# Attention weights turned by VectorE in blocks of 32 and placed by DMA over memory instead of by TensorE, key copies made by DMA, and eight weight sums moved to later units

## The chip, the cores and the metric

The kernel runs on one core of one Trainium2 chip. The metric is the device time of one execution in microseconds (us). A core has a matrix engine (TensorE, PE in the profile, with its weight loads shown apart as PEld), a vector engine (VectorE, DVE), a scalar engine (ScalarE, ACT), GpSimd (POOL), and SyncE (SP), which issues nearly all DMAs here. Each engine works through its own list of instructions strictly in order; an instruction that waits holds up all those behind it on that engine.

## What is computed

One encoder block on 512 positions of width 2048, in float32. The normalised input is projected once; half of the columns feed an attention of 16 heads of 64, the other half a gated linear attention of 4 heads. Both are gated, put together, projected again, added to the input and normalised. What matters here is the attention part, cut to its core:

```python
for window, dilation in DILATED_PATTERNS:      # (128,1), (512,4), (2048,16)
    o_p, lse_p = dilated_window_attention(aq, ak, av, rel_bias, window, dilation)
...
mix_w = jax.nn.softmax(jnp.stack(lses, axis=0), axis=0)
att = jnp.einsum('pbsh,pbshe->bshe', mix_w.astype(av.dtype), jnp.stack(outs, axis=0))
a_out = att.reshape(B, S, ATT_WIDTH) * jax.nn.silu(ag)
```

The three patterns merged by their denominators are one softmax over all 512 keys with a bias that depends on the distance alone, so for each head P = softmax(QK' + bias), a 512 x 512 matrix, and the output is P V.

## The kernel before

**Products.** A float32 product is made of three passes with rounded operands: each operand is split into a high part (ScalarE rounds it) and a low part (VectorE subtracts), and `three` (lines 169 to 171) does high x high, high x low and low x high. One call of `three`, three matmuls of 512 columns, is called a *tick* below.

**Units.** After a start stage the projection runs in *units* (`unit`): `qk2`, `qk4`, `qk6`, `gk`, `gv0`, `gv1`, `ag0`, `ag1`, `gg0`, `gg1`, then the output projection `o0` to `o3`. A unit has 64 ticks into four PSUM banks, in eight groups of eight, a group for each 512 KB of weights. A group's weights come by DMA into one of four `raw` buffers (line 286), ScalarE makes the high part (line 313) and VectorE the low part (line 297). `unit` takes a list of side work with places between 0 and 1; a piece is issued after the tick that its place names, and pieces with a place of 1 or more go to the next unit. TensorE's order is exactly the order of the code (`manual_schedule(engines={E.PE})`). The other engines' orders are chosen by the framework's scheduler when the program is built, piece by piece, among what it holds to be ready; side work is raised in priority (`urgent`).

**Attention as side work.** Four units (`qk2`, `qk4`, `qk6`, `gk`) carry four heads each, 16 tiles of 128 queries. Names in the orders below: `s13` are the scores of head 1, tile 3; `p13` its P; `pt01` the turned P of head 0, half 1 (tiles 2 and 3); `o01` the product of that half with V. For each tile:

- `score` (lines 567 to 587): two matmuls (576, 577), then VectorE adds the bias and takes the extreme (580), ScalarE the exponential with its sum (583), VectorE the reciprocal (584), GpSimd the scaling of P (585).
- `turn` (589 to 603): TensorE turns P against the identity in four 128 x 128 pieces (597) into a PSUM bank, ScalarE takes the high part (601), VectorE the low part (602), 512 columns each.
- `values` (605 to 619), once for two tiles: eight matmuls of 256 columns (611) with high and low part, a ScalarE copy (614), a VectorE addition into `cat` (618).

The side list is score x, turn x-1, values of the pair that ended with x-2, evenly spaced by `ATT_AT`. Scores, turned P and products share three PSUM banks.

**Keys.** At a unit's end `qk_evict` (line 531 on) takes queries and keys out of PSUM for the next unit's heads. A head's keys are wanted in both halves of the 128 partitions, so ScalarE copies the high part twice (548, 549) and VectorE makes the low part twice (550, 551), 64 x 512 each.

**Sums.** 48 pieces of weights (512 KB each, also through the `raw` buffers) are multiplied by a row and summed on VectorE (lines 244 and 680, about 1.3 us a piece). `SUMS_IN` says how many go into which unit; the rest fall into `gg1`.

## Time and profile before

| | |
|---|---|
| median of 3 runs | 975.26 us (973.75 to 977.06) |
| profiled execution, its own time | 973.38 us |
| span of its trace | 971.6 us |
| TensorE busy over the span | 943.0 us, 97% |
| VectorE, ScalarE, GpSimd busy | 616.6, 441.0, 81.6 us |
| first tick of `qk2` to first tick of `gv0` (four attention units) | 192.2 to 473.5 us |
| `gv0` and `gv1` | 473.5 to 580.6 us |

Times in the profile are from the span's start. A row of the timeline has start, duration, engine, line, operation, output and inputs; in brackets the idle time before it and what ended that. A matmul's duration is longer than its distance to the next one, since matmuls overlap: the distance of two starts is what one costs. The chain of waits counts that distance.

### The profile page before, as it was taken

The page shows a single profiled execution, that of the slowest core. Times are in us where ns is not written, and L with a number is a line of the kernel's source. Part 1 is how long each engine was busy: PE and PEld are TensorE (multiplying, and loading weights), DVE is VectorE, ACT ScalarE, POOL GpSimd, SP SyncE. Part 2 cuts the span into 40 slices and gives each one's busy share as a digit, 9 for nine tenths or more (in the row PEclk, how much of TensorE's full clock was granted, in tenths as well). Part 3 has the DMA queues.
Part 4 walks back from the last instruction along what each step waited for, and adds up shares of the span by engine and source line. Part 5 has one row for each costly group of instructions (what it writes and reads, how often), then busy time and mean ns, then how long its engine had stood idle before and what let it go on. Part 6 is the DMA issues. An engine that isn't in the chain of part 4 may idle for free.

```text
span 971.6 us, 11885 instructions
## 1 busy us (share of the span) xinstructions
PE 943.0 (97%) x4464; PEld 775.7 (80%) x4464; DVE 616.6 (63%) x916; ACT 441.0 (45%) x735; POOL 81.6 (8%) x100
## 2 busy tenths in 40 slices
PE   8999999989999999999999999999999999999996
PEld 4888788878778777778777888888888888888884
DVE  7988999566665676775534647585885352546431
ACT  5443533655655645655413544363744151333222
POOL 0000000011111122012000000000010000202120
PEclk9999999999999999999999999999999999999998
DMA  9998687422222253332444334355465455244013
GB/s 333 414 411 347 238 302 258 133 85 96 92 84 82 85 193 105 126 128 84 146 152 166 121 109 152 130 176 171 139 228 176 152 175 193 87 148 156 22 50 124
DMA packets 42619, 159.56 MB, mean 164 GB/s; under 512 B 5217, under 2 KB 5505, under 8 KB 37825
## 3 DMA queue, kind: packets, MB, share of 16 engines
q1 hardware_dynamic: 42386, 158.48, 47.2%
q8 instruction: 35, 0.57, 0.2%
q10 hardware_dynamic: 176, 0.33, 0.1%
q14 instruction: 22, 0.18, 0.1%
HBM read 154.51 MB, written 4.28 MB: 163 GB/s over the span
## 4 chain that ended last, share of the span: by engine, by line
PE 81%; DVE 8%; DMA 3%; ACT 3%; issue 3%; POOL 1%; SPq 0%; ACTq 0%; DVEq 0%; POOLq 0%
PE ps_o L170 6%; PE ps_o L171 6%; PE ps_o L169 6%; PE sta L169 3%; PE sta L170 3%; PE sta L171 3%; PE stb L171 3%; PE stb L169 3%; PE stb L170 3%; PE ps_qk L169 3%; PE ps_gv L170 3%; PE ps_gv L171 3%; PE ps_gv L169 3%; PE ps_qk L171 3%; PE ps_qk L170 3%
## 5 line engine op out<-in xcount | busy, mean ns | idle before, releaser
L585 POOL TENSOR_SCALAR p<-p,st 128x512 f32<-128x512 f32 x64 | 46.1, 721 | 424.3 <-DVE st L584 407.8
L583 ACT ACTIVATE p<-p,st 128x512 f32<-128x512 f32 x64 | 46.2, 722 | 63.4 <-DVE st L580 63.4
L244 DVE CUSTOM_DVE_ANT_0 cb<-cb,sb,c_bcond 128x2048 f32<-128x2048 f32 (+1 forms) x32 | 73.4, 2294 | 0.0
L602 DVE TENSOR_TENSOR pt<-t,pt 128x512 fp32r<-128x512 f32 x64 | 44.1, 689 | 17.8 <-ACT pt L601 17.8
L597 PE MATMUL t<-c_ident,p 128*128 128x128 f32 x256 | 38.9, 275 | 10.6 <-POOL p L585 10.6
L597 PEld LDWEIGHTS t<-c_ident,p 128*128 128x128 f32 x256 | 30.9, 140 | 22.3 <-POOL p L585 15.4
L580 DVE CUSTOM_DVE_ANT_0 p<-s,g 128x512 f32<-128x512 f32 x64 | 43.6, 686 | 7.0 <-PE s L577 6.1
L601 ACT ACTIVATE pt<-t 128x512 fp32r<-128x512 f32 x64 | 37.8, 591 | 21.1 <-PE t L597 20.5
L244 DVE CUSTOM_DVE_ANT_0 rawg<-rawg,sb,gate 128x1024 f32<-128x1024 f32 x16 | 20.7, 1294 | 27.8 <-DMA rawg<-in_wg 27.8
L611 PEld LDWEIGHTS o<-pt,vv 128*128 128x128 f32 x256 | 34.2, 189 | 3.8 <-DVE pt L602 1.7
L244 DVE CUSTOM_DVE_ANT_0 rawg<-rawg,sb,c_bcond 128x1024 f32<-128x1024 f32 x16 | 20.5, 1283 | 25.2 <-DMA rawg<-in_wg 25.2
L611 PE MATMUL o<-pt,vv 128*128 128x256 f32 x256 | 35.9, 283 | 0.0
L1014 POOL TENSOR_TENSOR x<-x,fgain 128x512 f32<-128x512 f32 x12 | 20.0, 1675 | 183.8 <-ACT ysq L1012 183.8
L1012 ACT ACTIVATE ysq<-x 128x512 f32<-128x512 f32 x16 | 10.1, 632 | 47.1 <-DVE x L1010 44.8
L767 POOL TENSOR_SCALAR dc<-st,sc 128x256 f32<-128x256 f32 x16 | 10.5, 656 | 242.5 <-DVE st L764 237.6
L584 DVE RECIPROCAL st<-st 128x1 f32<-128x1 f32 x64 | 10.4, 162 | 31.3 <-ACT p L583 31.2
L1009 DVE TENSOR_TENSOR y<-ps_o,sb 128x512 f32<-128x512 f32 x16 | 10.9, 684 | 25.9 <-PE ps_o L171 25.9
L576 PE MATMUL s<-ks,qs 128*128 128x512 f32 x64 | 25.3, 395 | 0.2 <-DVE qs L540 0.2
L577 PE MATMUL s<-kl,qs 128*128 128x512 f32 x64 | 25.0, 391 | 0.0
L774 ACT ACTIVATE sq<-st,sc 128x256 f32<-128x256 f32 x24 | 12.2, 509 | 26.2 <-DVE st L769 13.8
L618 DVE TENSOR_TENSOR cat<-o,oh 64x256 f32<-64x256 f32 x32 | 13.3, 415 | 11.9 <-ACT oh L614 11.7
L614 ACT ACTIVATE oh<-o 64x256 f32<-64x256 f32 x32 | 12.2, 380 | 17.3 <-PE o L611 16.5
(1279 smaller groups left out, 2944.6 us busy)
## 6 DMA issues: line engine op xcount, KB each, us to landing
cb<-in_wm SPq DMA_DIRECT2D x31, 1024.0 KB, 7.5
rawg<-in_wg SPq DMA_DIRECT2D x32, 512.0 KB, 3.4
raw_o<-in_w_o SPq DMA_DIRECT2D x32, 512.0 KB, 3.4
raw_qk<-in_w_qk SPq DMA_DIRECT2D x24, 512.0 KB, 3.3
rawb<-in_w_sb SPq DMA_DIRECT2D x16, 512.0 KB, 4.3
rawv<-in_wv SPq DMA_DIRECT2D x16, 512.0 KB, 3.4
raw_gv<-in_w_gv SPq DMA_DIRECT2D x16, 512.0 KB, 3.4
raw_ag<-in_w_ag SPq DMA_DIRECT2D x16, 512.0 KB, 3.4
```

What stands on the lines that cost most here:

```text
L169: mm(ps, lh, rh, start=first, stop=False)
L170: mm(ps, ll, rh, start=False, stop=False)
L171: mm(ps, lh, rl, start=False, stop=last)
L244: nc.vector.tensor_tensor_reduce(out=w, in0=w, in1=with_, op0=ALU.mult, op1=ALU.add, scale=1.0, scalar=init, accum_out=dst)
L576: mm(ps, qs[:, q], ks, start=True, stop=False)
L580: nc.vector.tensor_tensor_reduce(out=t, in0=ps, in1=gt[h][:, P * i:P * i + 512], op0=ALU.add, op1=ALU.min, scale=1.0, scalar=3e38, accum_o ...
L583: act(t, t, AF.Exp, bias=st[:, 0:1], scale=-1.0, accum_out=st[:, 1:2])
L585: nc.gpsimd.tensor_scalar(t, t, st[:, 2:3], 1.0, op0=ALU.mult, op1=ALU.mult)
L597: nc.tensor.transpose(pk[:, kt * P:kt * P + P], t[:, kt * P:kt * P + P], ident)
L601: act(hi, src, AF.Copy)
L602: tt(lo, src, hi.bitcast(F32), op=ALU.subtract)
L611: mm(po[:, :256], vv[h // 4][:, kt, h % 4, :], t[:, w, kt, :], start=kt == 0 and w == 0, stop=kt == 3 and w == 1)
```

## The change

1. `score` ends after the exponential. Reciprocal and scaling become a piece of their own, `scale`.
2. `turn` no longer uses TensorE. VectorE turns P in blocks of 32 x 32 within SBUF (STREAM_TRANSPOSE, 128 x 512), and SP writes the result to a buffer in memory (`away`, 256 KB a tile).
3. A new piece `back`, once for two tiles: four DMAs on SP read the buffer in such an order that the blocks land on the right partitions (`pf`, in a `raw` buffer; 128 KB each, in runs of 512 bytes). It waits for the two writes.
4. A new piece `parts`, once for two tiles: high part on ScalarE and low part on VectorE, 1024 columns each, out of SBUF.
5. The side list has places of its own for each piece of tile x, in steps of 0.0525 of a unit from 0.14 on: score at x, scale at x + 0.45, turn at x + 1.05; for a pair that ends with x: back at x + 1.9, parts at x + 3.1, values at x + 4.2. The values of a unit's last two pairs fall into the next unit.
6. The second copies of the keys (549, 551) become DMAs within SBUF on SP.
7. `SUMS_IN`: no sums in `qk6` and `gk` (4 each before); `gv0` 12 (9), `gv1` 5 (2), `ag0` 8 (7), `gg1` 5 (4). One more buffer of the `t2` pool, less scratch for DMAs.

```diff
-ATT_AT = (0.17, 0.8, 0.04, 0.05, 0.05)
+ATT_AT = (0.14, 0.0525)
-SUMS_IN = {"qk6": 4, "gk": 4, "gv0": 9, "gv1": 2, "ag0": 7, "ag1": 9, "gg0": 9}
+SUMS_IN = {"gv0": 12, "gv1": 5, "ag0": 8, "ag1": 9, "gg0": 9}
...
-            act(ks[oth], psk[own], AF.Copy)
+            nc.sync.dma_start(ks[oth].bitcast(F32), ks[own].bitcast(F32))
             tt(kl[own], psk[own], ks[own].bitcast(F32), op=ALU.subtract)
-            tt(kl[oth], psk[own], ks[own].bitcast(F32), op=ALU.subtract)
+            nc.sync.dma_start(kl[oth].bitcast(F32), kl[own].bitcast(F32))
...
                 act(t, t, AF.Exp, bias=st[:, 0:1], scale=-1.0, accum_out=st[:, 1:2])
+                pr_[h, i] = t, st
+            return go
+
+        def scale(h, i):
+
+            def go():
+                t, st = pr_.pop((h, i))
                 nc.vector.reciprocal(st[:, 2:3], st[:, 1:2])
                 nc.gpsimd.tensor_scalar(t, t, st[:, 2:3], 1.0, op0=ALU.mult, op1=ALU.mult)
...
         def turn(h, i):
             def go():
                 half, ii = divmod(i, 2)
-                if ii == 0:
-                    pt[h, half] = B8(f"pt{h}{half}", [2, 4, 256], F32R)
-                t = pr_.pop((h, i))
-                pk = PA(f"t{h}{i}")
-                for kt in range(4):
-                    nc.tensor.transpose(pk[:, kt * P:kt * P + P], t[:, kt * P:kt * P + P], ident)
...
+                t = T2(f"pt{h}{i}")
+                nc.vector.transpose(t.rearrange("p (b k r) -> p k b r", b=4, k=4), pr_.pop((h, i)))
+                nc.sync.dma_start(away[h, half][ii], t)
+            return go
+
+        def back(h, half):
+            def go():
+                t = away.pop((h, half))
+                f = RAW(f"pf{h}{half}", [8, 128])
+                for b in range(4):
+                    nc.sync.dma_start(f[32 * b:32 * b + 32], bass.AP(
+                        t.tensor, t.offset + P * b, [[512, 32], [32 * 512, 8], [1, P]]))
+                pf[h, half] = f
+            return go
+
+        def parts(h, half):
+            def go():
+                t = pt[h, half] = B8(f"pt{h}{half}", [2, 4, 256], F32R)
+                src = pf.pop((h, half)).rearrange("p b (k r) -> p k b r", k=4)
+                hi, lo = [t[:, e].rearrange("p k (b r) -> p k b r", b=8) for e in range(2)]
                 act(hi, src, AF.Copy)
                 tt(lo, src, hi.bitcast(F32), op=ALU.subtract)
...
+                items.append((x, score(*tiles[x])))
+                items.append((x + 0.45, scale(*tiles[x])))
+                items.append((x + 1.05, turn(*tiles[x])))
+                if tiles[x][1] % 2 == 1:
+                    h, half = tiles[x][0], tiles[x][1] // 2
+                    items.append((x + 1.9, back(h, half)))
+                    items.append((x + 3.1, parts(h, half)))
+                    items.append((x + 4.2, values(h, half)))
+        items.sort(key=lambda v: v[0])
```

**What stands in the orders.** First VectorE, around the low part of the pair `pt01` in the unit `qk2`. Before, from that low part to the addition of the pair's product:

```order
L602 TENSOR_TENSOR pt01_1643<-t03_1684,pt01_1643 128x4x128
L580 ISA p11_1704,st11_1705<-s11_1701,g1_1563 128x512
L580 ISA st11_1705 128x1
L602 TENSOR_TENSOR pt10_1714<-t10_1715,pt10_1714 128x4x128
L584 RECIPROCAL st11_1705<-st11_1705 128x1
L618 TENSOR_TENSOR cat0_1549<-o01_1725,oh01_1734 64x256
```

In the changed kernel, from the score that was issued last ahead of the pair's product to the addition:

```order
L580 ISA p13_1765,st13_1766<-s13_1762,g1_1573 128x512
L580 ISA st13_1766 128x1
L605 STREAM_TRANSPOSE pt12_1769<-p12_1730 128x4x4x32
L297 TENSOR_TENSOR qk26l_1854<-raw_qk26_1675,qk26h_1853 128x1024
L591 RECIPROCAL st13_1766<-st13_1766 128x1
L626 TENSOR_TENSOR pt01_1737<-pf01_1684,pt01_1737 128x1024
L642 TENSOR_TENSOR cat0_1549<-o01_1776,oh01_1785 64x256
```

The low part of `pt01` stood ahead of the bias pass of the score issued last before its product, and now stands behind that score's bias pass and its reciprocal, which needs that score's exponential. On ScalarE the high part of `pt01` stands in the same way right behind the exponential of `p13`.

Second TensorE, the same pair's product. Before, from the score issued last ahead of it:

```order
L577 MATMUL s11_1701<-kl01_1484,qs01_1474 128x512
L169 MATMUL ps_qk2_0_1509<-h_hi_150,qk23h_1609 128x512
L170 MATMUL ps_qk2_0_1509<-h_hi_150,qk23l_1610 128x512
L171 MATMUL ps_qk2_0_1509<-h_lo_151,qk23h_1609 128x512
L597 MATMUL t10_1715<-c_ident_1459,p10_1672 128x128 x4
L169 MATMUL ps_qk2_1_1510<-h_hi_150,qk23h_1609 128x512
L170 MATMUL ps_qk2_1_1510<-h_hi_150,qk23l_1610 128x512
L171 MATMUL ps_qk2_1_1510<-h_lo_151,qk23h_1609 128x512
L611 MATMUL o01_1725<-pt01_1643,vv0_921 128x256 x8
```

In the changed kernel:

```order
L577 MATMUL s13_1762<-kl01_1484,qs01_1474 128x512
L169 MATMUL ps_qk2_0_1509<-h_hi_150,qk24h_1672 128x512
L170 MATMUL ps_qk2_0_1509<-h_hi_150,qk24l_1673 128x512
L171 MATMUL ps_qk2_0_1509<-h_lo_151,qk24h_1672 128x512
L635 MATMUL o01_1776<-pt01_1737,vv0_921 128x256 x8
```

Between the score and the product there were two ticks and a turn; there is one tick now, and the product comes two scores later than before (after `s13`, not `s11`). Of the six products that a unit issues for its own pairs, five stand one tick behind a score and one stands right behind it. Of the two that fall into the next unit, the first stands three ticks after that unit's start, the second one tick behind its first score; in `gv0`, which has no scores, they stand after 3 and 10 ticks.

More of the change, by code (lines that the diff above doesn't have):

```diff
@@ L139, in block_kernel @@
     b8 = ctx.enter_context(tc.tile_pool(name="b8", bufs=8))
-    t2 = ctx.enter_context(tc.tile_pool(name="t2", bufs=15))
+    t2 = ctx.enter_context(tc.tile_pool(name="t2", bufs=16))
     gp = ctx.enter_context(tc.tile_pool(name="gp", bufs=2))
@@ L558, in attention @@
         tiles = [(2 * p + j, i) for p in pairs for j in range(2) for i in range(4)]
-        gt, pt, pr_ = {}, {}, {}
+        gt, pt, pr_, away, pf = {}, {}, {}, {}, {}
         heads = [2 * p + j for p in pairs for j in range(2)]
@@ L583, in go @@
                 act(t, t, AF.Exp, bias=st[:, 0:1], scale=-1.0, accum_out=st[:, 1:2])
+                pr_[h, i] = t, st
[3 more added lines that the diff above has]
+                t, st = pr_.pop((h, i))
                 nc.vector.reciprocal(st[:, 2:3], st[:, 1:2])
                 nc.gpsimd.tensor_scalar(t, t, st[:, 2:3], 1.0, op0=ALU.mult, op1=ALU.mult)
+                half, ii = divmod(i, 2)
+                if ii == 0:
+                    away[h, half] = dp.tile([2, P, 512], F32, tag=f"away{h}{half}", name=f"away{h}{half}")
                 pr_[h, i] = t
@@ L591, in go @@
                 half, ii = divmod(i, 2)
-                if ii == 0:
-                    pt[h, half] = B8(f"pt{h}{half}", [2, 4, 256], F32R)
-                t = pr_.pop((h, i))
-                pk = PA(f"t{h}{i}")
-                for kt in range(4):
-                    nc.tensor.transpose(pk[:, kt * P:kt * P + P], t[:, kt * P:kt * P + P], ident)
-                hi = pt[h, half][:, 0, :, P * ii:P * ii + P]
-                lo = pt[h, half][:, 1, :, P * ii:P * ii + P]
-                src = pk.rearrange("p (k q) -> p k q", k=4)
+                t = T2(f"pt{h}{i}")
[16 more added lines that the diff above has]
+                hi, lo = [t[:, e].rearrange("p k (b r) -> p k b r", b=8) for e in range(2)]
                 act(hi, src, AF.Copy)
@@ L622, in attention @@
         n = len(tiles)
-        for x in range(n + 3):
-            if x < n:
-                items.append(score(*tiles[x]))
-            if 1 <= x <= n:
-                items.append(turn(*tiles[x - 1]))
-            if 2 <= x <= n + 1 and tiles[x - 2][1] % 2 == 1:
-                items.append(values(tiles[x - 2][0], tiles[x - 2][1] // 2))
-        g_load(heads[0])
-        start, span, move0, move1, move_last = ATT_AT
-        at = [start + (q + 0.5) / len(items) * span for q in range(len(items))]
-        at[0] -= move0
-        at[1] -= move1
-        at[-1] += move_last
-        return list(zip(at, items))
+        for x in range(n):
+            if True:
+                items.append((x, score(*tiles[x])))
[7 more added lines that the diff above has]
+        items.sort(key=lambda v: v[0])
+        g_load(heads[0])
+        start, step = ATT_AT
+        return [(start + step * x, go) for x, go in items]
     def gate_half(m, z):
@@ L902, in block_kernel @@
     for n, p in (("qk2", 0), ("qk4", 2), ("qk6", 4)):
-        ps = unit(n, False, attention((p, p + 1)) + ([(0.05, shift_row)] + some_sums(n) if p == 4 else []))
+        ps = unit(n, False, attention((p, p + 1)) + ([(0.05, shift_row)] if p == 4 else []))
         for q in range(2):
             qk_evict(p + 2 + q, ps[2 * q], ps[2 * q + 1])
-    ps = unit("gk", False, attention((6, 7)) + some_sums("gk"))
+    ps = unit("gk", False, attention((6, 7)))
     gla["k"] = B8("gkt", [4, 512])
@@ L1119 @@
     nc = _bacc.Bacc("TRN2", target_bir_lowering=False, num_devices=1,
-                     dynamic_dma_scratch_size=4096)
+                     dynamic_dma_scratch_size=2048)
     aps = {}
```

## The prediction

> **What bounds the kernel now.** I read the page's busy times and chain first, then the attention stage by units, then single rows of that stage. Engine, busy time, share; then the chain that ended last:

> ```profile
> PE 943.0 (97%) x4464; PEld 775.7 (80%) x4464; DVE 616.6 (63%) x916; ACT 441.0 (45%) x735; POOL 81.6 (8%) x100
> PE 81%; DVE 8%; DMA 3%; ACT 3%; issue 3%; POOL 1%; SPq 0%; ACTq 0%; DVEq 0%; POOLq 0%
> ```

> TensorE sets the time. The four attention units, `gv0` and `gv1` by windows (stretch, length, busy time of PE, PEld, DVE, ACT, POOL, clock, DMA share, GB/s):

> ```profile
> 192.20:261.80 69.60, 65.98 (x346) 54.63 (x345) 45.95 (x94) 40.72 (x78) 11.08 (x16) 1.00 0.27 88
> ...
> 402.60:473.50 70.90, 67.55 (x353) 55.40 (x352) 47.71 (x98) 39.22 (x75) 11.09 (x16) 1.00 0.35 114
> 473.50:529.00 55.50, 55.04 (x245) 43.42 (x244) 22.39 (x28) 13.94 (x18) 0.00 (x0) 1.00 0.47 150
> 529.00:580.60 51.60, 51.60 (x261) 43.81 (x260) 30.98 (x40) 25.27 (x44) 1.91 (x4) 1.00 0.39 125
> ```

> In attention TensorE is nearly full, VectorE two thirds full. Its longest wait there, in total, count, longest:

> ```profile
> PE t L597 <- POOL p L585: 10.6, 11, 3.0
> ```

> The four units take 473.5 - 192.2 = 281.3 us, 70.3 each. What TensorE's own work costs, from the chain's pieces (four transposes; a pair's eight products) and the first two weight groups:

> ```profile
> 209.50 0.44 PE t L597 x4
> 213.61 0.95 PE o L611 x8
> L169 PE MATMUL ps_qk<-h_hi,qk20h x8: 388/390/390, 192.2 to 197.0; 128*128 128x512 f32 x8
> L169 PE MATMUL ps_qk<-h_hi,qk21h x8: 389/390/477, 197.7 to 207.4; 128*128 128x512 f32 x8
> L169 PE MATMUL ps_gv<-gv00h,h_hi x8: 388/390/397, 473.5 to 480.4; 128*128 128x512 f32 x8
> ```

> Eight ticks take 197.7 - 192.2 = 5.5 us, one 0.69, a unit's 64 ticks 44.0. A score is two matmuls, 0.46 by the starts below. A unit: 44.0 + 16 x 0.46 + 8 x 0.95 + 16 x 0.44 = 44.0 + 7.4 + 7.6 + 7.0 = 66.0. So 4.3 us a unit, 17 us in all, is waiting.

> **What goes.** TensorE's turning: 64 x 0.44 = 28.2 us on the bounding engine. Its own work is then 59.0 us a unit, 236.0 for four. The waits for GpSimd's P go with it.

> **What comes: a longer path to each product with V.** In the changed order the high and low parts of a pair stand behind the exponential and reciprocal of the score issued just ahead of the pair's product, and the product stands one tick behind that score. Engines work in order, so TensorE must wait until score, bias pass, exponential, high part and low part have gone through, one after the other. Rows of before give each link:

> ```profile
> 222.94 0.39 PE L577 MATMUL s<-kl,qs 128*128 128x512 f32 x1
> 223.17 0.39 PE L169 MATMUL ps_qk<-h_hi,qk23h 128*128 128x512 f32 x1
> 223.37 0.69 DVE L580 CUSTOM_DVE_ANT_0 p<-s,g 128x512 f32<-128x512 f32 x1 [0.85 <-PE s L577]
> 224.10 0.73 ACT L583 ACTIVATE p<-p,st 128x512 f32<-128x512 f32 x1 [2.03 <-DVE st L580]
> 224.73 0.19 ACT L583 ACTIVATION_READ_ACCUMULATOR p<-p,st 128x1 f32 x1
> ...
> 226.34 1.06 ACT L313 ACTIVATE qk26h<-raw_qk 128x1024 fp32r<-128x1024 f32 x1 [0.80 <-PE ps_qk L171]
> ...
> 227.44 1.22 DVE L297 TENSOR_TENSOR qk26l<-raw_qk,qk26h 128x1024 fp32r<-128x1024 f32 x1 [0.56 <-ACT qk26h L313]
> ...
> 228.58 0.16 DVE L584 RECIPROCAL st<-st 128x1 f32<-128x1 f32 x1
> ...
> 228.83 0.69 POOL L585 TENSOR_SCALAR p<-p,st 128x512 f32<-128x512 f32 x1 [2.86 <-DVE st L584]
> ```

> From the start of the score's second matmul to the end of the exponential's sum: 224.92 - 222.94 = 1.98. High part 1.06 (taken from L313, the same 1024 columns), hand-over 0.04 (227.40 to 227.44), low part 1.22 (L297), hand-over to TensorE 0.05: **4.35 us**. TensorE's own work in that time: the rest of the score 0.23, one tick 0.69, the first product on the high part 0.12 (0.95/8). It waits **3.3 us**. The reciprocal ends before the high part does and adds nothing.

> The product right behind its score lacks the tick: 4.0. A unit's last own pair also has the turning of tile 15 ahead of its low part: reciprocal, GpSimd (0.25 after the reciprocal's start, 0.69 long), turn, low part: 1.98 + 0.03 + 0.25 + 0.69 + 0.05 + 0.69 + 1.22 + 0.05 = 4.96, a wait of 3.9. For the 32 x 32 turn there is no row; I take a VectorE pass over 512 columns:

> ```profile
> L602 DVE TENSOR_TENSOR pt<-t,pt 128x512 fp32r<-128x512 f32 x64 | 44.1, 689 | 17.8 <-ACT pt L601 17.8
> L551 DVE TENSOR_TENSOR kl<-ps_qk,ks 64x512 fp32r<-64x512 f32 x12 | 8.3, 688 | 0.2
> L244 DVE CUSTOM_DVE_ANT_0 rawg<-rawg,sb,gate 128x1024 f32<-128x1024 f32 x16 | 20.7, 1294 | 27.8 <-DMA rawg<-in_wg 27.8
> ```

> 0.69 is the low end, 1.22 (the 1024-column pass) the high end.

> Of the pairs that fall into the next unit, the second again stands one tick behind a score: 3.3. The first stands behind the eviction: on VectorE ten passes lie between the last own pair's low part and its own, 7 x 0.69 + 0.42 + 2 x 1.22 = 7.7 us, some 9.5 with the ScalarE copies that alternate with them, against 0.95 + 6 x 0.69 = 5.1 of TensorE's: 2.6 to 4.5. The eviction of before shows such an alternation, a ScalarE copy that waits for a VectorE pass; I take 4.5:

> ```profile
> 266.53 0.59 ACT L539 ACTIVATE qs<-ps_qk 64x512 fp32r<-64x512 f32 x1 [1.38 <-DVE qs L540]
> ...
> L618 DVE TENSOR_TENSOR cat<-o,oh 64x256 f32<-64x256 f32 x32 | 13.3, 415 | 11.9 <-ACT oh L614 11.7
> ```

> In `gv0` no score stands ahead: about 1 us for both.

> Sum of new waits: 16 x 3.3 + 4 x 4.0 + 4 x 3.9 (own pairs) + 3 x 3.3 + 3 x 4.5 + 1 = **109 us**. That such a wait costs TensorE its full length, the start of `qk2` shows: ahead of the first turn it has nothing else to do.

> ```profile
> 203.58 0.39 PE L171 MATMUL ps_qk<-h_lo,qk21h 128*128 128x512 f32 x1
> 206.26 1.38 POOL L585 TENSOR_SCALAR p<-p,st 128x512 f32<-128x512 f32 x2 [205.82 <-DVE st L584]
> 207.00 0.44 PE L597 MATMUL t<-c_ident,p 128*128 128x128 f32 x2 [3.04 <-POOL p L585]
> ```

> **The sum.** 236.0 + 109 - 281.3 = +64 us against the profiled execution's 973.4 (span 971.6): 1037. That execution lies 1.9 under the median; against the median 975.3 + 64 = **1039 us**.

> **What costs nothing.** VectorE loses 64 low parts of 0.69, 16 second key copies and 8 sums, and gains 64 turns and 32 passes of 1.22: about 84 us for 65, in units that grow to 86 us each; hidden as long as those are bound by the path above. The moved sums, 8 x 1.3 = 10.4 us, meet 33 idle us of VectorE in `gv0` and 21 in `gv1`: nothing; at worst all 10. ScalarE loses more than it gains.

> The DMAs: a unit has 68 issues on SP (16 writes, 32 reads, 8 key copies, 12 others) at 0.33 us, 22 us. Issue, and landing of the nearest transfers:

> ```profile
> 226.90 0.33 SPq L564 DMA_DIRECT2D g<-grow  x1
> ...
> g<-grow SPq DMA_DIRECT2D x16, 448.0 KB, 4.0
> ...
> raw_gk<-in_w_gk SPq DMA_DIRECT2D x8, 512.0 KB, 3.4
> ...
> out<-x SPq DMA_DIRECT2D x16, 256.0 KB, 2.6
> ...
> lrb<-in_w_lr SPq DMA_DIRECT2D x1, 256.0 KB, 2.8
> ```

> `lrb` lands in 2.8 us although it comes in runs of 128 bytes; `pf` has runs of 512. In SP's order a pair's reads go out behind the write of the next pair's first tile, about 2.5 us ahead of TensorE's restart; the high part that needs them starts 2.3 us ahead of the next restart, and a pair takes 7 ticks, two scores, a product and a wait, 10.0 us. So there are 9.9 us for four issues and a landing, 1.3 + 4.0 = 5.3. Covered by 4.6 us. The low end of this cost is zero, since an earlier landing moves nothing.

> [...]

> **The rivals.** *Faster:* the wait does not occur, because the parts are through before TensorE arrives; it decides at a path of 4.35 us against 0.92 us of own work, so it needs five more ticks ahead of the product, or a scheduler's order that does not hold. For it: the code meant parts to come 1.1 steps ahead of the product, and waits of before vanish. Then 28.2 us go, and 0 to 17 of waiting: 930 to 947, say 938. Against: the order. Chance 0.09. In between, with most waits hidden, no change: 0.02.

> *DMA bound:* if the four reads land one after another at the 3.4 us of a whole load, they need 13.6 us against 9.9, and 24 pairs wait 3.7 us more: 1039 + 89 = 1128. For: 43,000 new packets (8,192 for the writes, 32,768 for the reads, 2,048 for the keys); against: `lrb`. Chance 0.06.

> *Slow clock:* TensorE starts slowly after a long idle time. At the program's start:

> ```profile
> 14.18 0.63 PE L169 MATMUL sta<-sa0h,h_hi 128*128 128x512 f32 x1
> 14.60 0.63 PE L170 MATMUL sta<-sa0h,h_lo 128*128 128x512 f32 x1
> ...
> 17.54 0.39 PE L171 MATMUL sta<-sa0l,h_hi 128*128 128x512 f32 x1
> 17.77 0.39 PE L169 MATMUL sta<-sa0h,h_hi 128*128 128x512 f32 x1
> ```

> Matmuls lie 0.42 apart, then 0.23; the 3.4 us between these rows hold eight and cost 8 x 0.19 = 1.5 us. After each of 30 waits that would be 45 us: 1084. Against: group `qk21`, in which the wait of 3.04 us falls, has a median matmul of 390 ns. My waits are slightly longer. Chance 0.06. [...]

> **The numbers.** Main case 0.77: 1039. Its own range: all links 0.4 us shorter and the eviction at 2.6 gives 92 us of waits, 1022; a turn of 1.22 (about 10 us more where VectorE is late) and half of the old waiting kept give 1058. I widen it to 1012 for a quicker low part, and to 1088 to hold the slow clock. Outside lie the faster rival, no change, DMA bound and 0.03 of the main case: 0.2. Faster by over 0.3% (about what a measurement of this kernel can tell from no change) 0.09, within 0.02, slower 0.89.

> **What would show it.** Right: attention units of 80 to 90 us; TensorE waiting at L635 for the low part L626 some 24 to 31 times, 3 to 4.5 us each; its share of the span under 90%; `gv0` on as before. Wrong: those waits missing or ended by a DMA; matmuls 0.42 apart after them; units under 66 us.

## The result and the profile after

The changed kernel takes **1098.6 us** (median of 4 runs, 1094.8 to 1103.0) against 974.5 us (4 runs) for the kernel before: ratio 1.128, 95% interval 1.1255 to 1.1302. It is slower, as forecast, but by 124 us and not by 64: 60 us over the forecast of 1039 and 10.6 us over the upper end of the range.

The page of the changed kernel, its first row of busy times and the row of the clock that TensorE was granted (40 slices of the span, tenths of full speed):

```profile
PE 976.4 (89%) x4208; PEld 793.7 (72%) x4208; DVE 643.1 (59%) x932; ACT 428.2 (39%) x687; POOL 88.6 (8%) x100
PEclk9999999979898888888887999999999999999998
```

TensorE has 256 instructions fewer and is busy longer, 976.4 us for 943.0. But for the last slice, the slices in which the clock is not full all lie in the stretch in which the attention runs.

The units by windows (stretch, length, busy time of PE, PEld, DVE, ACT, POOL, clock, DMA share, GB/s): `qk2`, `qk4`, `qk6`, `gk`, then `gv0` and `gv1`:

```profile
192.20:280.10 87.90, 69.40 (x274) 55.30 (x273) 49.03 (x94) 34.56 (x62) 13.26 (x16) 0.87 0.55 149
280.10:380.00 99.90, 73.85 (x290) 58.55 (x289) 50.97 (x96) 36.66 (x64) 13.24 (x16) 0.86 0.56 155
380.00:485.20 105.20, 78.53 (x290) 61.94 (x289) 50.98 (x96) 36.91 (x65) 13.25 (x16) 0.82 0.56 158
485.20:588.10 102.90, 76.69 (x289) 60.69 (x288) 48.91 (x93) 34.88 (x61) 13.24 (x16) 0.83 0.53 154
588.10:651.80 63.70, 56.06 (x242) 43.70 (x241) 29.69 (x38) 16.25 (x21) 0.00 (x0) 0.95 0.57 187
651.80:706.90 55.10, 54.36 (x271) 45.80 (x270) 36.25 (x50) 26.77 (x47) 1.91 (x4) 1.00 0.47 154
```

The four attention units take 395.9 us, 281.3 before: +114.6. `gv0` and `gv1` take 118.8 for 107.1: +11.7. All else is 1.1 shorter. The three sum to the 125.2 us by which the span grew (971.6 to 1096.8).

What TensorE waits for (in total, count, longest):

```profile
PE o L635 <- ACT pt L625: 69.6, 30, 4.0
PE o L635 <- DVE pt L626: 27.9, 30, 1.6
PE plr L948 <- DVE lrs L941: 6.3, 1, 6.3
...
PE ps_gv L169 <- ACT gkt L934: 1.3, 1, 1.3
```

Thirty products wait, each twice: for the high part, and after one matmul for the low part, 97.5 us together, 3.25 a product on average. Most wait 1.9 to 2.6 us and then 0.7 to 1.6; the first product after an eviction waits 3.9 to 4.0 and then 0.9. No product waits for a DMA. The wait for GpSimd's P is gone.

One such wait, from the timeline:

```profile
236.79 0.39 PE L577 MATMUL s<-kl,qs 128*128 128x512 f32 x1
237.21 0.69 DVE L580 CUSTOM_DVE_ANT_0 p<-s,g 128x512 f32<-128x512 f32 x1 [1.45 <-PE s L577]
...
238.01 0.72 ACT L583 ACTIVATE p<-p,st 128x512 f32<-128x512 f32 x1 [0.19 <-DVE st L580]
...
238.73 1.04 ACT L625 ACTIVATE pt<-pf 128x1024 fp32r<-128x1024 f32 x1
239.56 0.15 DVE L591 RECIPROCAL st<-st 128x1 f32<-128x1 f32 x1
239.80 1.22 DVE L626 TENSOR_TENSOR pt<-pf,pt 128x1024 fp32r<-128x1024 f32 x1
...
239.82 0.58 PE L635 MATMUL o<-pt,vv 128*128 128x256 f32 x1 [2.65 <-ACT pt L625]
241.08 1.86 PE L635 MATMUL o<-pt,vv 128*128 128x256 f32 x7 [0.68 <-DVE pt L626]
242.74 0.63 PE L169 MATMUL ps_qk<-h_hi,qk25h 128*128 128x512 f32 x1
...
243.17 0.63 PE L170 MATMUL ps_qk<-h_hi,qk25l 128*128 128x512 f32 x1
...
246.16 0.52 PE L171 MATMUL ps_qk<-h_lo,qk25h 128*128 128x512 f32 x1
246.51 0.40 PE L576 MATMUL s<-ks,qs 128*128 128x512 f32 x1
246.75 0.40 PE L577 MATMUL s<-kl,qs 128*128 128x512 f32 x1
```

Score, bias pass, exponential, high part, low part, product follow one another without a gap: 236.79 to 241.08, 4.29 us, forecast 4.35. What was not in the sum comes behind it: the product takes 1.86 us for seven matmuls, and the next nine matmuls lie 0.43 us apart; from 246.51 on they lie 0.23 apart again.

New and longer operations, from the groups (busy time, mean ns of one, idle time before):

```profile
L605 DVE STREAM_TRANSPOSE pt<-p 128x512 f32<-128x512 f32 x64 | 45.3, 707 | 5.5 <-POOL p L592 5.5
L626 DVE TENSOR_TENSOR pt<-pf,pt 128x1024 fp32r<-128x1024 f32 x32 | 39.3, 1227 | 13.5 <-ACT pt L625 12.8
L625 ACT ACTIVATE pt<-pf 128x1024 fp32r<-128x1024 f32 x32 | 33.3, 1041 | 0.8 <-DVE lrs L941 0.8
```

The turn costs 0.71 us, the low part 1.23, the high part 1.04, and no high part waits for a landing of `pf`.

So the attention units are made of 236.0 us of TensorE's own work by the forecast, 97.5 of waits, and 62.4 that are left. Most of the rest is the clock. The trace has it at half for 122.9 us of the units, 36 stretches of 3.41 us; in 12.6 of these TensorE idles, where the clock costs nothing, so it costs (122.9 - 12.6) / 2 = 55 us. About 7 us more are TensorE's own work at full clock: 61.4 to 61.7 us in each of the last three units, not 59.0. A likely reason, an estimate from the rows above: a matmul with a wait behind it counts to the end of its row, 0.39 us, and not just to the next start, 0.23. That this makes up the 7 us is argued, not shown.

### The profile page after: what moved, and what is told of

Its sections match the earlier page's. It is cut to its first block, busy times and chain, and to the rows that moved or that the text cites. A ratio compares the mean times of both kernels' runs of the same rounds, so it can differ in the third digit from the quotient of the medians.

```text
span 1096.8 us, 11811 instructions
## 1 busy us (share of the span) xinstructions
PE 976.4 (89%) x4208; PEld 793.7 (72%) x4208; DVE 643.1 (59%) x932; ACT 428.2 (39%) x687; POOL 88.6 (8%) x100
## 2 busy tenths in 40 slices
DMA packets 89212, 197.32 MB, mean 180 GB/s; under 512 B 8801, under 2 KB 41857, under 8 KB 84417
## 4 chain that ended last, share of the span: by engine, by line
PE 45%; DVE 4%; ACT 3%; issue 2%; DMA 2%; POOL 0%; ACTq 0%; DVEq 0%; SPq 0%
PE ps_o L171 5%; PE ps_o L170 5%; PE ps_o L169 5%; PE ps_ag L169 3%; PE ps_ag L171 3%; PE ps_ag L170 3%; PE ps_gv L169 2%; PE ps_gv L170 2%; PE ps_gv L171 2%; PE ps_gg L169 2%; PE ps_gg L171 2%; PE ps_gg L170 2%; PE go L829 2%; PE o L635 1%; PE ps_gk L169 1%
## 5 line engine op out<-in xcount | busy, mean ns | idle before, releaser
L635 PE MATMUL o<-pt,vv 128*128 128x256 f32 x256 | 63.9, 392 | 97.4 <-ACT pt L625 69.6
L635 PEld LDWEIGHTS o<-pt,vv 128*128 128x128 f32 x256 | 49.0, 267 | 116.9 <-ACT pt L625 82.2
L592 POOL TENSOR_SCALAR p<-p,st 128x512 f32<-128x512 f32 x64 | 53.0, 828 | 527.6 <-DVE st L591 413.8
L580 DVE CUSTOM_DVE_ANT_0 p<-s,g 128x512 f32<-128x512 f32 x64 | 44.2, 690 | 84.7 <-PE s L577 84.5
L583 ACT ACTIVATE p<-p,st 128x512 f32<-128x512 f32 x64 | 46.2, 722 | 112.8 <-DVE st L580 111.8
L244 DVE CUSTOM_DVE_ANT_0 cb<-cb,sb,c_bcond 128x2048 f32<-128x2048 f32 (+1 forms) x32 | 73.4, 2294 | 0.0
L605 DVE STREAM_TRANSPOSE pt<-p 128x512 f32<-128x512 f32 x64 | 45.3, 707 | 5.5 <-POOL p L592 5.5
L626 DVE TENSOR_TENSOR pt<-pf,pt 128x1024 fp32r<-128x1024 f32 x32 | 39.3, 1227 | 13.5 <-ACT pt L625 12.8
L244 DVE CUSTOM_DVE_ANT_0 rawg<-rawg,sb,gate 128x1024 f32<-128x1024 f32 x16 | 20.5, 1283 | 26.6 <-DMA rawg<-in_wg 26.6
L625 ACT ACTIVATE pt<-pf 128x1024 fp32r<-128x1024 f32 x32 | 33.3, 1041 | 0.8 <-DVE lrs L941 0.8
L791 POOL TENSOR_SCALAR dc<-st,sc 128x256 f32<-128x256 f32 x16 | 10.4, 649 | 258.1 <-DVE st L788 252.9
L244 DVE CUSTOM_DVE_ANT_0 rawg<-rawg,sb,c_bcond 128x1024 f32<-128x1024 f32 x16 | 20.7, 1293 | 17.3 <-DMA rawg<-in_wg 17.3
L577 PE MATMUL s<-kl,qs 128*128 128x512 f32 x64 | 25.2, 393 | 0.0
L798 ACT ACTIVATE sq<-st,sc 128x256 f32<-128x256 f32 x24 | 12.2, 508 | 24.3 <-DVE st L788 12.6
L1034 DVE TENSOR_TENSOR x<-y,x 128x512 f32<-128x512 f32 x16 | 18.0, 1126 | 0.3
## 6 DMA issues: line engine op xcount, KB each, us to landing
away<-pt SPq DMA_DIRECT2D x64, 256.0 KB, 2.1
rawg<-in_wg SPq DMA_DIRECT2D x32, 512.0 KB, 3.5
raw_o<-in_w_o SPq DMA_DIRECT2D x32, 512.0 KB, 3.3
raw_qk<-in_w_qk SPq DMA_DIRECT2D x24, 512.0 KB, 3.9
rawb<-in_w_sb SPq DMA_DIRECT2D x16, 512.0 KB, 4.5
raw_gv<-in_w_gv SPq DMA_DIRECT2D x16, 512.0 KB, 4.1
```

Source lines behind the costliest of these rows:

```text
L244: nc.vector.tensor_tensor_reduce(out=w, in0=w, in1=with_, op0=ALU.mult, op1=ALU.add, scale=1.0, scalar=init, accum_out=dst)
L580: nc.vector.tensor_tensor_reduce(out=t, in0=ps, in1=gt[h][:, P * i:P * i + 512], op0=ALU.add, op1=ALU.min, scale=1.0, scalar=3e38, accum_o ...
L583: act(t, t, AF.Exp, bias=st[:, 0:1], scale=-1.0, accum_out=st[:, 1:2])
L592: nc.gpsimd.tensor_scalar(t, t, st[:, 2:3], 1.0, op0=ALU.mult, op1=ALU.mult)
L605: nc.vector.transpose(t.rearrange("p (b k r) -> p k b r", b=4, k=4), pr_.pop((h, i)))
L625: act(hi, src, AF.Copy)
```

## The experiments

**The theory** after the result: (a) the orders of the engines force a wait at each product; (b) TensorE's idling halves its clock for the matmuls behind. **Rivals:** the transfers (89212 packets in the changed kernel, 42619 before) set the pace; or their traffic, not the idling, slows the matmuls; or the keys' copies and the moved sums cost. Time is that of the run, "units" the four attention units. The runs e1_fill, e1_fill14, e2_short, e3_order and e6_double are single executions; four of the changed kernel spread over 8 us.

| run | time, us | units, us | waits at the products, us | clock in the units |
|---|---|---|---|---|
| before | 974.5 | 281.3 | none | 1.00 |
| changed | 1098.6 | 395.9 | 97.5 | 0.84 |
| e1_fill | 1055.8 | 352.1 | 11.6 | 1.00 |
| e1_fill14 | 1070.2 | 364.3 | 52.4 | 0.96 |
| e2_short | 1040.3 | 343.6 | 63.2 | 0.89 |
| e3_order | 1024.3 | 319.6 | 52.0 | 0.93 |
| e3c_later | 993.9 | 293.2 | 39.6 | 0.95 |
| e4_boundary | 983.3 | 279.6 | 18.5 | 0.98 |
| e5_eviction | 983.5 | 280.6 | 18.3 | 0.96 |
| e5b_eviction | 976.6 | 284.9 | 20.9 | 0.95 |
| e6_double | 1123.3 | 424.3 | 125.9 | 0.82 |
| keys_alone | 966.2 | 272.0 | none | 1.00 |
| sums_alone | 971.9 | 278.8 | none | 0.99 |
| keys_sums | 961.2 | 267.2 | none | 1.00 |

### Is it the idling that slows the matmuls? (e1_fill, e1_fill14)

```diff
                 po = PA(f"o{h}{half}")
+                for _ in range(28):
+                    mm(po[:, 256:512], h_hi[:, 0, :P], h_hi[:, 0, :256], start=True, stop=True)
```

> The changed kernel, and ahead of each product with V 28 matmuls of 256 columns on operands that are always at hand, into the unused half of the product's PSUM bank (work added, result unused); at the 0.12 us that a product's matmul costs, 3.3 us, about the wait. Theory: waits forced by the orders, 97 us, and behind each a stretch in which TensorE has half its clock, about 65 us in all by the mean granted clock (0.938 against 0.997). TensorE then has nothing idle: the stretches vanish, the waits turn into dummy work (32 x 3.3 = 106 us for 97), about 1042 us, granted clock back at 0.99. Rival, the slow stretches come from the transfers' traffic: they stay, 1099 to 1107 us. Rival, the transfers set the pace: 1099 us.

Measured: 1055.8 us. With 28 dummy matmuls a product, windows row of the units and waits:

```profile
192.40:544.50 352.10, 340.50 (x1979) 300.22 (x1979) 199.00 (x379) 143.16 (x252) 53.15 (x64) 1.00 0.60 172
```

```profile
PE o L637 <- DVE pt L626: 9.5, 18, 0.9
PE o L637 <- ACT pt L625: 2.1, 4, 1.4
```

TensorE does some 100 us of useless work (840 matmuls in the units at 0.12 us each) where it idled 97.5, and the program is 43 us *faster*: the clock is 1.00 with the same transfers, moved in a shorter time (172 GB/s for 149 to 158). The traffic is not what slows the matmuls; the idling is. Against the expected 1042 it is 14 us more, mostly since the slow stretches cost 55 us and not 65.

With 14 dummies in place of 28:

> As the run with 28 dummy matmuls ahead of each product, with 14: 1.65 us of the wait are filled, 0.3 to 1.0 us ahead of the first matmul of a product and 0.9 behind it stay idle. Theory, after the first four runs: the clock is set anew every 3.41 us, and halves if TensorE idled for more than about 1.5 to 1.9 us of the last such stretch. Then nearly all slow stretches go though TensorE still waits, and no work is added beyond the wait: the changed kernel's 1098.6 less 62 us, 1035 to 1045 us, shorter than with 28. Rival, every interruption brings the slow clock: it stays near 0.94, 1090 to 1100 us. Rival, the slow stretch needs a whole stretch without work: none would have been there in the changed kernel, and filling changes nothing, 1099 us.

Measured: 1070.2 us at 0.96 in the units, between the theory and its rivals. Both rivals fall (the clock does recover, and it recovers though 52 us of waits stay), but "nearly all" was too much, since the waits are not all alike. Where 0.3 us or less stay ahead of a product's first matmul, none of 17 products is followed by a slow stretch; where 0.7 to 1.0 us stay, 5 of 8 are; where more, 3 of 5.

### What makes the slow stretch? (e2_short)

```diff
-                    items.append((x + 3.1, parts(h, half)))
-                    items.append((x + 4.2, values(h, half)))
+                    items.append((x + 4.1, parts(h, half)))
+                    items.append((x + 4.95, values(h, half)))
```

> The changed kernel with the parts at x + 4.1 and the product at x + 4.95: three ticks now lie between a score and the product, the parts still stand behind that score's exponential. Theory: the wait falls from 3.3 us to 4.35 - 0.23 - 3 x 0.69 - 0.12 = 1.9 us, 40 us less in all, and with shorter waits most of the slow stretches go (up to 65 us): 995 to 1010 us. If only the wait shortens and the slow stretches stay: 1058 us. Rival, transfers set the pace: 1099 us, and the wait would end on a DMA.

Measured: 1040.3 us. The waits shrank nearly as expected:

```profile
PE o L635 <- ACT pt L625: 33.7, 26, 4.2
PE o L635 <- DVE pt L626: 29.5, 30, 1.8
```

63 us for 57. But the clock rose only to 0.89. Two products of this run, in the timeline, with the same two waits of 0.61 and 0.87 us:

```profile
224.13 0.39 PE L635 MATMUL o<-pt,vv 128*128 128x256 f32 x1 [0.61 <-ACT pt L625]
225.39 1.10 PE L635 MATMUL o<-pt,vv 128*128 128x256 f32 x7 [0.87 <-DVE pt L626]
...
226.88 0.63 PE L169 MATMUL ps_qk<-h_hi,qk24h 128*128 128x512 f32 x1
...
229.86 0.50 PE L170 MATMUL ps_qk<-h_hi,qk24l 128*128 128x512 f32 x1
230.20 0.40 PE L171 MATMUL ps_qk<-h_lo,qk24h 128*128 128x512 f32 x1
...
240.12 0.49 PE L170 MATMUL ps_qk<-h_hi,qk25l 128*128 128x512 f32 x1
240.45 0.39 PE L171 MATMUL ps_qk<-h_lo,qk25h 128*128 128x512 f32 x1
...
251.94 0.39 PE L635 MATMUL o<-pt,vv 128*128 128x256 f32 x1 [0.61 <-ACT pt L625]
253.20 1.10 PE L635 MATMUL o<-pt,vv 128*128 128x256 f32 x7 [0.87 <-DVE pt L626]
254.13 0.40 PE L576 MATMUL s<-ks,qs 128*128 128x512 f32 x1
254.37 0.40 PE L577 MATMUL s<-kl,qs 128*128 128x512 f32 x1
```

Behind the first the clock halves, not at the wait's end but over 1 us later (the rows from 226.88 on), and is full again at 230.1; the next slow stretch ends at 240.3, 10.2 = 3 x 3.41 us later. Behind the product at 251.94 nothing is slow. The granted clock of the interval of each product and of the next one (stretch, length, busy time of PE, PEld, DVE, ACT, POOL, clock, DMA share, GB/s):

```profile
223.27:226.68 3.41, 1.93 (x12) 1.44 (x11) 1.98 (x3) 0.90 (x2) 1.78 (x1) 1.00 0.82 265
226.68:230.09 3.41, 3.41 (x10) 2.64 (x9) 1.81 (x5) 1.10 (x3) 0.69 (x1) 0.50 0.83 182
250.57:253.99 3.42, 1.94 (x11) 1.27 (x10) 1.47 (x3) 1.31 (x3) 0.69 (x1) 1.00 0.72 212
253.99:257.40 3.41, 3.41 (x18) 2.84 (x17) 1.71 (x4) 1.75 (x3) 0.00 (x0) 1.00 1.03 214
```

So the slow stretches keep to a grid of their own. In five traces (the changed kernel, e1_fill14, e2_short, e3_order, e3c_later) the trace's own clock has 77 slow stretches (without those at the programs' two ends), and in each trace all of them end on one grid of 3.413 us, within 0.01 us. Adding up TensorE's idle time ahead of its rows in each interval of the grid, from `qk2` to the end of `gv1`:

| idle in an interval of 3.41 us | next at full clock | next at half clock |
|---|---|---|
| interval at full clock, idle under 1.45 us | 475 (342 without idling) | 0 |
| 1.45 to 2.0 us | 23 | 26 |
| 2.0 us and more | 0 | 51 |
| interval at half clock, idle under 0.5 us | 76 | 0 |
| 0.5 to 0.7 us | 1 | 2 |
| 0.7 us and more | 0 | 19 |

The other nine traces agree: at full clock no interval of 958 with under 1.45 us of idling is followed by half clock, and all 35 with 2.0 us or more are. So in these traces 2.0 us or more of idling within an interval at full clock was always followed by half clock (51 of 51 and 35 of 35), in one piece (2.29 us in the changed kernel's interval from 212.29 us) or several (2.42 us, of which 1.46 in one piece, in that from 502.42), and at half clock 0.7 us or more kept it there (19 of 19). No interval had to be idle throughout. Between 1.45 and 2.0 us both followed, and in e2_short it went by where in the interval the idling lies. Twelve intervals of that run hold just the two waits above, 1.48 us: the eight in which these begin within 0.60 us of the interval's start are followed by half clock, the four in which they begin 0.76 us or later are not. Why the place goes with it stays open.

### Is the wait forced by the order? (e3_order, e3c_later)

```diff
+    fence = {}
+    def behind(engine):
+        return tc.issue_after(fence[engine].ins) if fence else nullcontext()
...
+                with behind("DVE"):
                     nc.vector.tensor_tensor_reduce(
...
+                with behind("ACT"):
                     act(t, t, AF.Exp, bias=st[:, 0:1], scale=-1.0, accum_out=st[:, 1:2])
...
-                act(hi, src, AF.Copy)
-                tt(lo, src, hi.bitcast(F32), op=ALU.subtract)
+                fence["ACT"] = act(hi, src, AF.Copy)
+                fence["DVE"] = tt(lo, src, hi.bitcast(F32), op=ALU.subtract)
```

> The changed kernel with its places, but a score's bias pass is forced behind the low part issued ahead of it in the code, and its exponential behind the high part. Theory: the wait for that score's exponential goes; what is left is the landing of the turned P. From a score to the landing: bias, exponential, scaling and turn some 5 us after the next score's start, write 3, four reads 5.2, 13.3 in all, the high part could start 11.6 after it, so about 1.7 us a pair are left, 54 us: about 990 us if the slow stretches go with the long waits, 1055 if they stay. TensorE's waits then end on high or low parts that themselves waited for the landing. Rival, transfers set the pace already: 1099 us.

Measured: 1024.3 us. Only edges between instructions of one engine were added, and 74 us went. The waits are 52.0 us, 54 expected:

```profile
PE o L641 <- DVE pt L632: 28.6, 30, 1.4
PE o L641 <- ACT pt L631: 23.4, 21, 2.2
```

Now the landing shows, as expected; ScalarE's waits name it:

```profile
ACT pt L631 <- DMA pf<-away: 11.5, 10, 3.3
```

The time, 1024.3, lies between the two cases expected (990 and 1055), and the clock, 0.93, is only in part back. The same with parts and product later:

```diff
-                    items.append((x + 3.1, parts(h, half)))
-                    items.append((x + 4.2, values(h, half)))
+                    items.append((x + 4.1, parts(h, half)))
+                    items.append((x + 5.4, values(h, half)))
...
-    lrb = B8("lrb", [KT, 32])
+    lrb = T2("lrb").rearrange("p (k c) -> p k c", c=32)
```

> As the run before, with the parts at x + 4.1 and the product at x + 5.4, two ticks behind the next score: the low part stands behind the bias pass of score x + 4, ahead of that of score x + 5. The load of the small low-rank weights takes a buffer of another pool, so that the pairs that fall into gv0 have room. Theory: product due 17.3 us after its first score, all links 17.1 us: no forced wait, no slow stretch; TensorE's own 236 us for the four units and up to 15 of small waits: 930 to 950 us, faster than the kernel before at 974.5. Rival, transfers set the pace: 1050 us and more. Rival, the traffic slows the matmuls: about 995 us at a granted clock of 0.94.

Measured: 993.9 us (987.5 to 995.7), ratio to the kernel before 1.018 (1.0132 to 1.0227): 105 us better than the changed kernel, not faster than before, where 930 to 950 us were expected. The windows row of `qk2`, then of the three other units together:

```profile
192.20:251.10 58.90, 56.81 (x265) 46.58 (x264) 43.82 (x85) 30.25 (x55) 11.46 (x15) 1.00 0.68 186
251.10:485.40 234.30, 198.90 (x867) 159.41 (x866) 152.91 (x291) 109.51 (x193) 35.46 (x48) 0.93 0.74 203
```

`qk2` runs in 58.9 us with hardly a wait: the turning and the old waits are gone. It is not a full unit, though: three of its eight products fall into the next one (265 matmuls here, 288 in a full unit), so the forecast's own work for it is 59.0 - 3 x 0.95 = 56.2 us, and 2.1 us of it TensorE idles. The other units take 78 us. At each boundary products wait, the worst for a landing:

```profile
275.02 1.06 ACT L631 ACTIVATE pt<-pf 128x1024 fp32r<-128x1024 f32 x1 [2.98 <-DMA pf<-away]
276.11 1.23 DVE L632 TENSOR_TENSOR pt<-pf,pt 128x1024 fp32r<-128x1024 f32 x1 [2.81 <-ACT pt L631]
276.13 0.39 PE L641 MATMUL o<-pt,vv 128*128 128x256 f32 x1 [3.75 <-ACT pt L631]
```

The reads behind it were issued from 265.6 on, among two loads of `g` and three of weights, and landed after 7.5 us (3.3 in the changed kernel). The time is also that of the rival in which the traffic slows the matmuls (995 us). But here too only idling is followed by the slow clock: each of this trace's nine full-clock intervals with 1.99 us of idling or more is, and none with less.

### Can the boundary be mended? (e4_boundary, e5_eviction, e5b_eviction)

```diff
+                    more = {n - 5: (0, 1.0), n - 3: (1.5, 1.7), n - 1: (2.2, 2.6)}.get(x, (0, 0))
-                    items.append((x + 4.1, parts(h, half)))
-                    items.append((x + 5.4, values(h, half)))
+                    items.append((x + 4.1 + more[0], parts(h, half)))
+                    items.append((x + 5.4 + more[1], values(h, half)))
```

> As the kernel with the order forced and the product at x + 5.4, with the three pairs at a unit's end later: product of the pair that ends with tile 11 by 1.0 step, parts and product of tile 13's pair by 1.5 and 1.7 steps, of tile 15's by 2.2 and 2.6, so that they no longer stand inside the eviction and its loads. Theory: what is left against the kernel before are the waits at the units' boundaries, 4 to 9 us and their slow stretches for each of four; they go: 940 to 955 us, faster than the kernel before at 974.5. Rival, the transfers at a unit's start (pf landing in 7.5 us beside loads) hold up the chain wherever the product stands: 980 to 995 us.

Measured: 983.3 us, ratio 1.009 (1.0069 to 1.0114): a miss, in the range of the rival. The products' waits fell to 18.5 us, and the next one appeared, which ends with an eviction and not with a landing:

```profile
PE ps_qk L169 <- DVE qs L540: 8.1, 4, 3.5
```

TensorE waits for a PSUM bank: with its work shorter, the eviction is what is late, behind turns and low parts on VectorE. Two tries to put it ahead:

```diff
+                late = x == n - 1
-                items.append((x + 1.05, turn(*tiles[x])))
+                items.append((x + 1.05 + late * 0.6, turn(*tiles[x])))
...
-                    more = {n - 5: (0, 1.0), n - 3: (1.5, 1.7), n - 1: (2.2, 2.6)}.get(x, (0, 0))
+                    more = {n - 5: (0, -0.3, 1.0), n - 3: (0, 1.5, 1.9), n - 1: (0.7, 2.4, 3.0)}.get(x, (0, 0, 0))
+                    items.append((x + 1.9 + more[0], back(h, half)))
```

> As the run with the boundary pairs moved, and now the eviction goes ahead of the attention's pieces at a unit's end: the parts of tile 11's pair 0.3 step earlier, scaling unchanged, turn and reads of tile 15 by 0.6 and 0.7 steps later, parts and product of tile 13's pair by 1.5 and 1.9, of tile 15's by 2.4 and 3.0. Theory: at a boundary TensorE waits 3.5 us for a bank whose eviction stands behind a turn that itself waits for GpSimd and behind a low part; with the eviction ahead that goes, and the slow stretch behind it: the attention units come from 280 us to 255 to 265, the whole to 958 to 970 us, at or under the kernel before. Rival, transfers at the unit's start bind: unchanged, 980 to 986 us.

Measured: 983.5 us, ratio 1.010 (1.0072 to 1.0124), a miss: the wait for the bank is now 4.7 to 6.0 us at each of the three boundaries between attention units. The early parts wait for their landing (1.6 us at the first), and the bias pass of the unit's last score and the eviction stand behind them.

```diff
-                    more = {n - 5: (0, -0.3, 1.0), n - 3: (0, 1.5, 1.9), n - 1: (0.7, 2.4, 3.0)}.get(x, (0, 0, 0))
+                    more = {n - 5: (0, 1.7, 1.9), n - 3: (0, 1.5, 1.9), n - 1: (0.7, 2.4, 3.0)}.get(x, (0, 0, 0))
...
+    lrb = T2("lrb").rearrange("p (k c) -> p k c", c=32)
+    nc.sync.dma_start(lrb, a["w_lr"][0])
     ps = unit("gk", False, attention((6, 7)))
```

> Second try at the units' boundaries: as the run e5_eviction, but the parts of tile 11's pair 1.7 steps later and its product 1.9 later, into the next unit, where the eviction is issued ahead of them (in the first try the bias pass of the unit's last score, and the eviction behind it, stood behind these parts, and they behind a late landing); the low-rank weights are loaded at the start of gk. Theory: the boundary waits of 4.7 to 6.0 us and the 5.1 us wait in gv0 go, with their slow stretches: 983.5 less 20 to 30 us, 953 to 965 us, no slower than the kernel before with keys and sums alone (961). Rival, the eviction on VectorE and ScalarE is simply too long beside the pieces of the attention: 975 to 985 us.

Measured: 976.6 us, ratio 1.003 (1.0008 to 1.0046). The wait in `gv0` went, and the gain is there: the four units themselves take 284.9 us, 280.6 in the first try. Their boundary waits are spread over more and smaller ones, none for a bank over 1.8 us. It is the rival's figure, if at its lower end. This is the best version with the turn on VectorE that I found. It is about even with the kernel before, and 15 us behind keys_sums below, which has the same keys and sums and leaves the turning on TensorE.

### The two smaller parts (keys_alone, sums_alone, keys_sums)

In the kernel before, only the keys' copies as DMAs (the change's own four lines), or only the table:

```diff
-SUMS_IN = {"qk6": 4, "gk": 4, "gv0": 9, "gv1": 2, "ag0": 7, "ag1": 9, "gg0": 9}
+SUMS_IN = {"qk6": 0, "gk": 0, "gv0": 12, "gv1": 5, "ag0": 8, "ag1": 9, "gg0": 9}
```

> The kernel before with only the second copies of the keys as DMAs. Theory and prediction: nothing, 973 to 977 us. Rival, the first score of a unit waits for the copies to land (2.2 us each, eight issues of 0.46 us): up to 4 us a unit, 985 to 990 us.

Measured: 966.2 us, ratio 0.992 (0.9896 to 0.9952): faster.

> The kernel before with only the new table of sums (none in qk6 and gk; gv0 12, gv1 5, ag0 8, gg1 5). Prediction: nothing, 973 to 977 us, at worst 10 us more. Rival, the sums of gv0 and gv1 delay the splits of weights there, which would explain the 12 us that these two units lost: 980 to 987 us.

Measured: 971.9 us, ratio 0.997 (0.9956 to 0.9985): a little faster. Neither costs anything in the kernel before, so the loss is hardly theirs; no run has the turning without them. Both together:

> The kernel before with the keys' second copies as DMAs and the new table of sums, without the turning by VectorE. If the gains of the two runs alone (7.7 and 2.1 us) add up: 964 us, faster than both kernels. If both come from the same relief of VectorE and ScalarE at a unit's end: 966 us.

Measured: **961.2 us**, ratio 0.987 (0.9847 to 0.9885), faster than both kernels. The gains add up and a little more. TensorE's longest wait of before has nearly gone (10.6 us, 11 times, in the kernel before):

```profile
PE t L597 <- POOL p L585: 2.1, 5, 0.7
```

### More transfers (e6_double)

```diff
                 pf[h, half] = f
+                g = dp.tile([P, 8, P], F32, tag=f"again{h}{half}", name=f"again{h}{half}")
+                for b in range(4):
+                    nc.sync.dma_start(g[32 * b:32 * b + 32], bass.AP(
+                        t.tensor, t.offset + P * b, [[512, 32], [32 * 512, 8], [1, P]]))
```

> The changed kernel with each of the four reads of a pair issued twice, the second time from the same buffer to another place in memory that nothing uses: twice the reads' traffic and issues on SP. Theory: the landing is not what TensorE waits for in the changed kernel (4.6 us of cover by the prediction), 1095 to 1110 us, and no engine waits for a landing of pf. Rival, the transfers set the pace or slow the matmuls: 1130 us and more.

Measured: 1123.3 us, 25 more, between theory and rival, and not a clean test: the edit also changed the scheduler's order, and at a unit's end the parts of tile 11's pair came to stand behind the eviction:

```profile
280.31 0.58 PE L639 MATMUL o<-pt,vv 128*128 128x256 f32 x1 [8.06 <-ACT pt L629]
```

The waits at products in the units grew by 27 us in all (95.2 and 29.6), most of it at the units' ends. Inside the units a product's two waits come to 2.7 to 4.0 us, against 2.8 to 3.5 in the changed kernel, and ScalarE waits for `pf` 4.5 us in all, where the theory had no such wait. That speaks for the theory inside the units, in the main; what the added traffic costs at the boundaries stays open.

## Why the prediction was right and wrong

- **What goes: nearly right.** The pieces gave 66.0 us of own work a unit; the units of keys_sums, with hardly a wait, take 66.8 on average. Without the turning 59.0 was forecast; between waits at full clock the changed kernel's full units take 61.4 to 61.7. The prediction's own windows rows show that less than the 4.3 us a unit that it calls waiting was idle: 3.6 us in `qk2`, 3.4 in `gk`.
- **The forced path: right, in mechanism and nearly in size.** Path 4.35 us (4.29 measured), on average 3.4 us a product (109/32; 3.25 measured for 30), 109 us in all (97.5). The forecast counted by starts, so its wait holds the ends of the matmuls ahead as well: own work and waits together were put at 345.0 us and came to 340.8. e3_order shows the cause, since the order alone was changed and almost half of the wait went with it. Its signs hold in part: the low part was waited for 30 times, but 1.6 us at most, as the longer half of each wait ended with the high part; only `qk2` fell into 80 to 90 us a unit, and matmuls 0.42 us apart, a sign of being wrong, were seen.
- **The slow clock: this step failed.** The sum 236.0 + 109 - 281.3 has no term for it, and it cost 55 us. It stood as a rival at 0.06, set aside because a single wait of 3.04 us left no trace in the kernel before. But in these traces the clock did not go by a wait's length: it went by how much idling fell into one interval of the grid (under 1.45 us none of 475 was followed by half clock, from 2.0 us on all 51 were). The slow stretch at that program's start ends at about 17.5 us; an estimate, 55 intervals of 3.413 on, puts a boundary at 205.2, in the midst of the wait from 203.96 to 207.00, which leaves 1.2 and 1.8 us on its sides, the one under 1.45, the other in the band in which either happened (23 and 26). So by this estimate the row that the prediction argued from had, by luck, a harmless place on the grid. Of the changed kernel's 30 waiting products (2.0 to 2.7 us and then 0.7 to 0.9 for most, a short matmul between), 25 bring a slow stretch. e1_fill shows that idling is the cause. Size: 55 us and not the 45 of the rival. Its 1.5 us for each interval was right (55/36 = 1.5); but 11 of the 25 stretches last two intervals, since idling of 0.6 us and more within the first kept the clock at half, so there are 36 intervals and not 30.
- **DMAs covered: right for the changed kernel**, though four issues took 1.8 us and not 1.3: no high part waits for `pf`. (The 9.9 us of room do not come out of their terms, which give 2.5 + 10.0 - 2.3 = 10.2; nothing hangs on it.) Right only as long as the forced wait hides them: e3_order and e3c_later lay the landing bare, 7.5 us at a boundary against 4.0 taken. The changed kernel's median landing was 3.3 us.
- **`gv0` on "as before": wrong by 11.7 us.** Most of it is a wait of 6.3 us for the low-rank weights: their load stands behind the last pair's reads in SP's list, and these wait 5.6 us there for the low part of a weight group in `gv0`. A wait of 1.3 us, one product more than before (0.95) and some 2.4 us of half clock make 11.0.
- **Keys and sums "nothing": wrong in sign.** They gain 13 us in the kernel before (keys_sums), mostly by taking away waits that the forecast had already struck out for the changed kernel. That they bring no second gain there is argued; no run has the changed kernel without them.
- **The sum with the measured terms:** 236.0 + 97.5 + 62.4 - 281.3 = 114.6, and 11.7 - 1.1 for the rest: 125.2 us between the two profiled spans. The upper end, 1088, was set to hold the rival's 1084; the slow clock in its true size, 1039 + 55 = 1094, lies beyond even without `gv0`.

## What to carry to other kernels

Taking 28 us off the bounding engine is worth nothing if the piece that replaces them is put where the scheduler sets it behind the next tile's work: read each engine's order around the consumer, and fix it by an explicit edge if it has to hold. Price a wait of TensorE at its length and at the half-speed interval that can follow as well: in five traces here 1.45 to 2.0 us of idling within one interval of 3.41 us at full clock brought one in 26 of 49 cases, 2.0 us and more in 51 of 51; there even useless matmuls paid (1098.6 to 1055.8 us). And run the small companions of a large change by themselves: here they were the only gain (961.2 us without the turn, 976.6 with it in its best form).
